# A hybrid decoder block on one core: head norms by transposes and row sums instead of a product with ones, and three sets of operands for the output's blocks

## The chip, the core and the metric

The kernel runs on one core of a Trainium2 chip. The metric is the device time of one execution in microseconds (us); the median of three runs is compared. TensorE is PE in the profile (PEld is its loading of stationary operands), VectorE DVE, ScalarE ACT, GpSimd POOL, and SyncE SP, which here only issues DMAs. Each engine takes its instructions in the order in which they stand in its queue.

## What is computed

One decoder block over 1024 tokens of 1024 channels, all in float32. After an RMSNorm, one input projection gives queries, keys, values and gates for two groups of heads. Eight heads of 64 channels do stick-breaking attention, four heads of 128 do a gated delta rule in chunks. Each head's output is normalised over its own channels, multiplied by a gate, and all of it goes through the output projection, a residual sum and a last RMSNorm. The change concerns the norm of the attention's heads and the output projection:

```python
o_sb = stick_breaking_attention(to_heads(sb_q, SB_HEADS, SB_HEAD_DIM), ...)
o_sb = rmsnorm(o_sb.transpose(0, 2, 1, 3), sb_norm_w[layer]).reshape(b, t_len, SB_WIDTH)
o_sb = o_sb * jax.nn.silu(sb_z)
...
mixed = jnp.concatenate([o_sb, o_gdn], axis=-1)
x = x + jnp.einsum('bte,ed->btd', mixed, w_out[layer])
return rmsnorm(x, final_norm_w)
```

Here rmsnorm(x, w) is x / sqrt(mean(x * x) + 1e-6) * w, the mean taken over the 64 channels of a head.

## The kernel before

**A planner sets the order.** The program is written as twelve generators (streams): projections, the four steps of the delta rule, attention, the output's weights, `factors`, `prepare`, `product` and others. `interleave` (L394) runs a model of the engines (class `Model`, L139) while the program is recorded: whenever TensorE's queue is empty in the model, it lets the ready stream of lowest priority number go on to its next `yield`. A stream yields either a condition (`lambda`) or an operation whose end it needs. So TensorE's queue is in the order of recording, and the queues of the other engines are in the order in which the model starts their instructions, by priority; both are fixed in the program (L1436 to L1439). Any change of an operation, a priority or a condition can move everything behind it. All operations pass through one recorder, so that the profile has the line L316 for nearly all of them and they are told apart by their tiles.

**Precision.** Large products are made of three passes (`mm3`, L517) over operands that are split in a high and a low part (xh and xl, weh and wel, woh and wol, mh and ml); their moving operand has up to 512 columns. The small products and the transposes take float32 operands as they are.

**Attention.** Heads are taken in pairs that share 128 partitions (64 rows of a tile each), and queries in pairs of blocks of 128 tokens. `pair(h, p)` (L1191) transposes the weights sg on TensorE with the identity (`ident`, a part of the tile step), multiplies them by the values into the bank po, and puts the output of head h for 256 tokens into half of the tile oe (128 rows of channels by 256 tokens) and into DRAM (o_s). After the second head of a pair (h odd) oe is squared on ScalarE, and a product with `sel` (128 x 128, two columns of ones over 64 rows each, the rest is not used for sums) gives the sums of squares over each head's 64 rows in two rows of a bank of the ring pz. VectorE turns them into mean plus epsilon in oe[0:2], and a DMA puts these two rows into DRAM (ss_s). That happens 16 times: four head pairs, four pairs of blocks.

**The factors.** `factors` (L1259) waits for a head pair's last sums (for the last head pair: for each pair of blocks), reads them from DRAM spread over 128 partitions (sst), takes the inverse square root by ten small steps on VectorE (`_rsqrt`, L45), and writes them back to DRAM (rs_s). That happens seven times: head pairs 0 to 2 once each with 16 columns, head pair 3 four times with 4 columns.

**The output stage.** It works on eight blocks of 128 tokens. `prepare` (L1336) makes a block's operands in two halves. The delta half (g = 1) transposes mx, the normed delta output that `mixed_delta` scaled on VectorE, and multiplies it by its gate. The attention half (g = 0) loads o_s (oa), the factors with a broadcast over 64 partitions (rb) and the gates (ga), multiplies rb by the gates on GpSimd (the fourth head pair's gate is still on chip as zt), and multiplies oa by that on VectorE (mf). Both halves end in mh (ScalarE) and ml (GpSimd). The operands of a block and its residual rows xr lie in one of two sets, in turn, so that block b waits for the end of block b - 2 (`f{b - 2}`, L1342). `product` (L1374) multiplies each block by the output weights in two parts of 512 columns (the last block in three) and eight slices of channels, adds the residual, and norms the result. The first two blocks' delta halves are multiplied before their attention halves. The output weights' rows 0 to 3 are split (woh, wol) once the last projection is done, since they lie where its operands were.

**Small things.** The constants conv, n1, mixw and others lie in the unused columns of sel. The delta group keeps its factors in rk, rq and rsg.

## Time and profile before

| | |
|---|---|
| median of three runs | 678.75 us (678.58 to 679.62) |
| the profiled execution's own time | 679.42 us |
| its span, first to last instruction | 677.6 us |
| TensorE busy | 655.8 us, 97% |
| VectorE busy | 480.1 us, 71% |
| ScalarE busy | 381.7 us, 56% |
| GpSimd busy | 327.0 us, 48% |
| DMA, mean share of the 16 engines | 47.1% |

A row of the profile that groups instructions has line, engine, operation, out<-in, shapes and count, then the time in which at least one of them ran, the mean duration in ns, and the idle time of the engine just ahead of them with what ended it. A row of a timeline has start and length in us, engine, line, operation, tiles, shape and count; a square bracket holds idle time ahead and its releaser. Matmuls are pipelined: one's duration overlaps the next, so what it costs the queue is the distance between starts.

### The profile page before, as it was taken

The page shows a single profiled execution, that of the slowest core. Times are in us where ns is not written, and L with a number is a line of the kernel's source. Part 1 is how long each engine was busy: PE and PEld are TensorE (multiplying, and loading weights), DVE is VectorE, ACT ScalarE, POOL GpSimd, SP SyncE. Part 2 cuts the span into 40 slices and gives each one's busy share as a digit, 9 for nine tenths or more (in the row PEclk, how much of TensorE's full clock was granted, in tenths as well). Part 3 has the DMA queues.
Part 4 walks back from the last instruction along what each step waited for, and adds up shares of the span by engine and source line. Part 5 has one row for each costly group of instructions (what it writes and reads, how often), then busy time and mean ns, then how long its engine had stood idle before and what let it go on. Part 6 is the DMA issues. An engine that isn't in the chain of part 4 may idle for free.

```text
span 677.6 us, 11750 instructions
## 1 busy us (share of the span) xinstructions
PE 655.8 (97%) x3998; PEld 557.8 (82%) x3998; DVE 480.1 (71%) x1007; ACT 381.7 (56%) x953; POOL 327.0 (48%) x301
## 2 busy tenths in 40 slices
PE   8999999999899989999999999999999999999995
PEld 6889987897788878788877888888888888877884
DVE  5354646425997866997598898997879964786643
ACT  5663138824797654966777684677858531322121
POOL 0002157527943677523797249863446444334331
PEclk9999999999899999999999999999999999999999
DMA  8928253546060555045433237253264755477431
GB/s 302 387 91 319 94 189 124 182 155 201 20 203 19 137 153 164 2 140 154 135 123 103 80 91 237 68 157 99 82 192 133 253 173 156 136 220 229 134 130 63
DMA packets 80972, 102.17 MB, mean 151 GB/s; under 512 B 17584, under 2 KB 49680, under 8 KB 80912
## 3 DMA queue, kind: packets, MB, share of 16 engines
q1 hardware_dynamic: 80912, 101.42, 47.1%
q8 instruction: 32, 0.52, 0.3%
q14 instruction: 28, 0.23, 0.1%
HBM read 73.50 MB, written 27.89 MB: 150 GB/s over the span
## 4 chain that ended last, share of the span: by engine, by line
PE 67%; POOL 12%; DVE 7%; ACT 5%; issue 5%; DMA 3%; SPq 1%; POOLq 0%; ACTq 0%; DVEq 0%
PE pp L316 39%; PE pz L316 19%; PE po L316 6%; POOL tm L316 6%; PE pc L316 3%; POOL wel L316 2%; POOL sg L316 2%; ACT pz L316 1%; DMA rb<-rs_s 1%; DVE cc L316 1%; DVE pp L316 1%; DVE pre L316 1%; ACT sg L316 1%; POOL kq L316 1%; SPq L316 1%
## 5 line engine op out<-in xcount | busy, mean ns | idle before, releaser
L316 PE MATMUL pp<-xh,weh 128*128 128x512 f32 x384 | 160.3, 417 | 3.8 <-DVE pre L316 3.8
L316 PE MATMUL pp<-xh,wel 128*128 128x512 f32 x384 | 151.0, 393 | 0.0
L316 PE MATMUL pp<-xl,weh 128*128 128x512 f32 x384 | 150.5, 392 | 0.0
L316 POOL TENSOR_TENSOR sg<-sg,cc 128x128 f32<-128x128 f32 (+3 forms) x64 | 77.1, 1209 | 63.6 <-DVE cc L316 37.2
L316 POOL TENSOR_TENSOR wel<-wer,weh 128x512 fp32r<-128x512 f32 x48 | 62.1, 1295 | 88.9 <-ACT weh L316 83.2
L316 PEld LDWEIGHTS pp<-xh,weh 128*128 128x128 f32 x384 | 72.4, 188 | 16.5 <-DVE pre L316 5.9
L316 PEld LDWEIGHTS pp<-xh,wel 128*128 128x128 f32 x384 | 72.2, 188 | 16.3
L316 PEld LDWEIGHTS pp<-xl,weh 128*128 128x128 f32 x384 | 72.6, 189 | 10.3
L316 POOL TENSOR_TENSOR tm<-xs,br 128x32 f32<-128x32 f32 (+7 forms) x64 | 59.2, 925 | 12.3 <-DVE xs L316 11.2
L316 ACT ACTIVATE ah<-pz 128x512 fp32r<-128x512 f32 (+1 forms) x80 | 43.5, 556 | 31.7 <-PE pz L316 30.8
L316 ACT ACTIVATE sg<-pz,sel 128x384 f32<-128x384 f32 (+3 forms) x96 | 53.8, 589 | 10.4 <-PE pz L316 9.3
L316 DVE TENSOR_TENSOR al<-pz,ah 128x512 fp32r<-128x512 f32 (+1 forms) x80 | 49.7, 630 | 10.3 <-ACT ah L316 9.9
L316 DVE TENSOR_TENSOR_SCAN cc<-pz,step 128x384 f32<-128x384 f32 (+2 forms) x64 | 53.1, 844 | 4.9 <-ACT pz L316 2.3
L316 ACT ACTIVATE pz<-pz,sel 128x384 f32<-128x384 f32 (+3 forms) x96 | 52.4, 565 | 0.1
L316 PE MATMUL pp<-chl,xh 128*128 128x264 f32 (+1 forms) x256 | 47.0, 285 | 0.8 <-DVE pre L316 0.8
L316 PE MATMUL pz<-step,sg 128*128 128x128 f32 x288 | 43.8, 275 | 2.4 <-DVE cc L316 1.7
L316 PE MATMUL po<-ah,v2a 128*128 128x256 f32 (+1 forms) x160 | 43.7, 297 | 0.0
L316 POOL TENSOR_TENSOR ml<-mf,mh 128x512 fp32r<-128x512 f32 x16 | 20.6, 1291 | 46.0 <-ACT mh L316 46.0
L316 DVE SCALAR_TENSOR_TENSOR pp<-pre,sel,pp 128x512 f32<-128x512 f32 x48 | 36.0, 749 | 9.6 <-ACT pp L316 8.9
L316 DVE TENSOR_REDUCE xs<-tm 128x16 f32<-128x32 f32 (+7 forms) x64 | 27.7, 432 | 18.5 <-POOL tm L316 18.0
L316 PEld LDWEIGHTS pp<-chl,xh 128*128 128x128 f32 x256 | 39.6, 188 | 1.2 <-DVE pre L316 1.0
L316 PE MATMUL pp<-woh,mh 128*128 128x512 f32 (+1 forms) x104 | 39.6, 381 | 0.6 <-ACT mh L316 0.6
(254 smaller groups left out, 1599.1 us busy)
## 6 DMA issues: line engine op xcount, KB each, us to landing
wer<-wE SPq DMA_DIRECT2D x48, 256.0 KB, 3.2
xr<-x SPq DMA_DIRECT2D x16, 512.0 KB, 8.6
qk_s<-xq SPq DMA_DIRECT2D x8, 512.0 KB, 4.8
v_s<-v2e SPq DMA_DIRECT2D x16, 256.0 KB, 2.0
q<-qk_s SPq DMA_DIRECT2D x8, 512.0 KB
kh<-qk_s SPq DMA_DIRECT2D x8, 512.0 KB
kl<-qk_s SPq DMA_DIRECT2D x8, 512.0 KB, 5.1
v2a<-v_s SPq DMA_DIRECT2D x8, 512.0 KB, 8.7
```

Of the source, the lines that this page charges most:

```text
L316: ins = f(*args, **kw).ins
```

## The change

The sums of squares: the product with sel, VectorE's evacuation of two rows and the DMA to ss_s go. In their place the squared oe is transposed in two pieces of 128 tokens, and one reduction on VectorE sums the 64 channels of each head and block into a tile that stays on chip, ssn (128 tokens by head pair, block and head). `factors` adds the mean and epsilon there, takes the inverse square root as before, transposes the result on TensorE (16 or 4 rows of 128 tokens), copies it out of the bank and writes it to rs_s. The load from ss_s goes.

```diff
                 sp = pz()[:, 0:256]
-                TE.matmul(sp, sel, oe, start=True, stop=True)
-                V.tensor_scalar(oe[0:2], sp[0:2], 1.0 / SBD, EPS, ALU.mult, ALU.add)
-                flags[f"t{h // 2}{p}"] = S.dma_start(ss_s[h // 2, p], oe[0:2])
+                for u in range(2):
+                    TE.transpose(sp[:, u * P:(u + 1) * P], oe[:, u * P:(u + 1) * P], ident)
+                flags[f"t{h // 2}{p}"] = V.tensor_reduce(ssn[:, h // 2, 2 * p:2 * p + 2, :].rearrange("p b u -> p (b u)"),
+                                                         sp.rearrange("p (n d) -> p n d", d=SBD), AX.X, ALU.add)
...
-                yield S.dma_start(ss, src)
-                _rsqrt(V, None, rs, ss, m, us)
-                r = S.dma_start(dst, rs)
+                ss = ssn[:, j, bl, :].rearrange("p b u -> p (b u)")
+                rs, us = rst[:, 0:m], ust[:, 0:m]
+                V.tensor_scalar(ss, ss, 1.0 / SBD, EPS, ALU.mult, ALU.add)
+                yield _rsqrt(V, None, rs, ss, m, us)
+                yield lambda: ps.room("pz", 4)
+                tp = pz()
+                TE.transpose(tp[0:m, 0:P], rs, ident)
+                V.tensor_copy(rsn[0:m], tp[0:m, 0:P])
+                r = S.dma_start(rs_s[j, bl].rearrange("b u t -> (b u) t"), rsn[0:m])
```

The output's blocks: a third set of operands lies in the tiles v2a and cc of attention. Block b waits for the end of block b - 3 instead of b - 2 (block 2 for the loaded last gain fnw instead of the end of block 0). A block's first product also waits, while the program is recorded, for attention's last output.

```diff
-                    yield lambda: b == 0 or "late" in flags and (b < 2 or f"f{b - 2}" in flags)
-                    pool = (pools[0], at_)[b % 2]
-                    xr = pool.tile([P, D], F32, **(dict(tag="cc", bufs=2) if b % 2 else dict(tag="xr")), name="xr")
+                    yield lambda: b == 0 or "late" in flags and (b < 2 or "fnw" in flags and (b < 3 or f"f{b - 3}" in flags))
+                    pool = at_ if b % 3 else pools[0]
+                    xr = pool.tile([P, D], F32, **(dict(tag="cc", bufs=2) if b % 3 else dict(tag="xr")), name="xr")
                     S.dma_start(xr, x_d[bs, :])
-                    mh = pool.tile([P, NK, P], F32R, tag=("mh", "kl")[b % 2], name="mh")
-                    ml = pool.tile([P, NK, P], F32R, tag=("ml", "q2")[b % 2], name="ml")
+                    mh, ml = [pool.tile([P, NK, P], F32R, tag=t, bufs=1 + (t == "v2a"), name="mh") for t in (("mh", "ml"), ("kl", "q2"), ("v2a", "v2a"))[b % 3]]
...
-                        yield lambda: ps.room(tag, bufs)
+                        yield lambda: f"e{SBH - 1}{NB // 2 - 1}" in flags and ps.room(tag, bufs)
```

The low part ml is now also named mh in the program's names. The rest makes room: sel becomes small (the constants alone, without memset and reduction), sst, ss_s, rsg and rk go; the delta group's last scaling is written into rq in place, and its key factor rr takes the place of mr2b, with nk computed ahead of mr2b.

How the queues move. TensorE, around the sums of the last head pair's last blocks (oe is the squared output, pp a projection's bank). Before:

```order
2519 L316 MATMUL pp_6731<-xl_109,weh_6561 128x512
2520 L316 MATMUL pp_6731<-xh_108,wel_6562 128x512
2521 L316 MATMUL pz_6761<-oe_6628,sel_66 128x256
2522 L316 MATMUL pp_6731<-xh_108,weh_6561 128x512
2523 L316 MATMUL pp_6731<-xl_109,weh_6561 128x512
2524 L316 MATMUL pp_6731<-xh_108,wel_6562 128x512
```

And now, where the transpose of the factors from these sums (rst) follows at row 2600:

```order
2573 L316 MATMUL pp_6846<-xl_105,weh_6716 128x512
2574 L316 MATMUL pp_6846<-xh_104,wel_6717 128x512
2575 L316 MATMUL pz_6876<-step_65,oe_6698 128x128 x2
2576 L316 MATMUL pp_6846<-xh_104,weh_6716 128x512
2577 L316 MATMUL pp_6846<-xl_105,weh_6716 128x512
2578 L316 MATMUL pp_6846<-xh_104,wel_6717 128x512
```

One product has become two transposes; between rows 2575 and 2600 stand 24 matmuls of projections.

TensorE in the output stage, at the transposes of block 2's delta half (mx; woh, wol with mh, ml are output products, po and pc the banks of block 0, pz that of block 1). Before:

```order
2689 L316 MATMUL pc_7028<-woh2_6981,ml_6658 128x512
2690 L316 MATMUL pc_7028<-woh3_6985,mh_6657 128x512
2691 L316 MATMUL pc_7028<-wol3_6986,mh_6657 128x512
2692 L316 MATMUL pc_7028<-woh3_6985,ml_6658 128x512
2693 L316 MATMUL pz_7112<-step_65,mx_6991 128x128 x4
2694 L316 MATMUL pz_7041<-woh0_6973,mh_6686 128x512
2695 L316 MATMUL pz_7041<-wol0_6974,mh_6686 128x512
2696 L316 MATMUL pz_7041<-woh0_6973,ml_6687 128x512
```

Now:

```order
2672 L316 MATMUL pz_7075<-woh6_6552,mh_6801 128x512
2673 L316 MATMUL pz_7075<-woh7_6577,mh_6800 128x512
2674 L316 MATMUL pz_7075<-wol7_6578,mh_6800 128x512
2675 L316 MATMUL pz_7075<-woh7_6577,mh_6801 128x512
2676 L316 MATMUL pz_7092<-step_65,mx_7012 128x128 x4
2677 L316 MATMUL po_7036<-woh0_6994,mh_6702 128x512
2678 L316 MATMUL po_7036<-wol0_6995,mh_6702 128x512
2679 L316 MATMUL po_7036<-woh0_6994,mh_6703 128x512
```

The four transposes stood behind the second half of block 0's products; they now stand ahead of it, 24 matmuls earlier.

SP's queue, at the last store of factors (rs_s) and the loads of block 2's attention half (the oa, rb and ga that follow the three pairs mx and gt). Before:

```order
377 L316 DMA gt_7008<-gate_s_91 128x4x128
378 L316 DMA rs_s_94<-rst_75 128x4
379 L316 DMA oa_7129<-o_s_92 128x4x128
380 L316 DMA rb_7130<-rs_s_94 64x4x128 x2
381 L316 DMA ga_7131<-gate_s_91 128x3x128
382 L316 DMA xr_7108<-x 128x1024
```

Now, with block 2's oa_7109, rb_7110 and ga_7111 next behind the last row:

```order
344 L316 DMA rs_s_90<-rsn_75 4x128
345 L316 DMA oa_6947<-o_s_89 128x4x128
346 L316 DMA rb_6948<-rs_s_90 64x4x128 x2
347 L316 DMA ga_6949<-gate_s_88 128x3x128
348 L316 DMA mx_7012<-og_s_91 128x512
349 L316 DMA fnw_7010<-fnw 128x1024
350 L316 DMA gt_7013<-gate_s_88 128x4x128
351 L316 DMA mx_7020<-og_s_91 128x512
352 L316 DMA gt_7021<-gate_s_88 128x4x128
353 L316 DMA mx_7028<-og_s_91 128x512
354 L316 DMA gt_7029<-gate_s_88 128x4x128
355 L316 DMA xr_7088<-x 128x1024
```

The store stood directly ahead of block 2's loads and now stands ahead of block 1's.

More of the change, by code (lines that the diff above doesn't have):

```diff
@@ L452, in block @@
         ident = step[:, 384:512]
-        sel = cst.tile([P, P], F32, name="sel")
-        conv = sel[:, 2:50].rearrange("p (a b) -> p a b", b=4)
-        n1, mixw, rstd, rs8, ns8, al2 = [sel[:, 50 + 8 * i:58 + 8 * i] for i in range(6)]
+        small = cst.tile([P, 96], F32, name="small")
+        conv = small[:, 0:48].rearrange("p (a b) -> p a b", b=4)
+        n1, mixw, rstd, rs8, ns8, al2 = [small[:, 48 + 8 * i:56 + 8 * i] for i in range(6)]
         alog, dtb = al2[:, 0:GH], al2[:, GH:]
@@ L458, in block @@
         make_identity(nc, ident)
-        V.memset(sel[:, 98:P], 0.0)
-        V.tensor_reduce(sel[:, 0:2], ident.rearrange("p (h d) -> p h d", h=2), AX.X, ALU.add)
-        sst, rst, ust = [cst.tile([P, 16], F32, name=n) for n in ("sst", "rst", "ust")]
+        rst, ust = [cst.tile([P, 16], F32, name=n) for n in ("rst", "ust")]
+        ssn = cst.tile([P, 4, NB, 2], F32, name="ssn")
+        rsn = cst.tile([16, P], F32, name="rsn")
         V.memset(step[:, 0:384], 0.0)
-        rsg = cst.tile([P, GH, NB], F32, name="rsg")
         ssg = cst.tile([P, GH, NB], F32, name="ssg")
-        rk = cst.tile([P, GH, NB], F32, name="rk")
         rq = cst.tile([P, GH, NB], F32, name="rq")
@@ L1261, in factors @@
                 yield from until(f"t{j}{p}")
+                bl = slice(0, NB) if j < 3 else slice(2 * p, 2 * p + 2)
                 m = 16 if j < 3 else 4
[L1263 to L1267 removed]
+                ss = ssn[:, j, bl, :].rearrange("p b u -> p (b u)")
[7 more added lines that the diff above has]
+                r = S.dma_start(rs_s[j, bl].rearrange("b u t -> (b u) t"), rsn[0:m])
                 for b in range(NB) if j < 3 else (2 * p, 2 * p + 1):
```

17 lines of the change are left out of this document (7 added, 10 removed).

## The prediction

> **What bounds the kernel now.** I read the page's first part, then the busy time by stretches, then the waits, and last the timeline of each engine around the two places that the change touches.
>
> ```profile
> PE 655.8 (97%) x3998; PEld 557.8 (82%) x3998; DVE 480.1 (71%) x1007; ACT 381.7 (56%) x953; POOL 327.0 (48%) x301
> ```
>
> ```profile
> 260.00:280.00 20.00, 19.79 (x146) 15.99 (x145) 16.62 (x29) 15.37 (x38) 12.32 (x11) 1.00 0.33 101
> 340.00:360.00 20.00, 19.18 (x106) 15.48 (x105) 19.22 (x32) 13.09 (x27) 19.31 (x16) 1.00 0.50 158
> ...
> 580.00:600.00 20.00, 20.00 (x92) 16.29 (x91) 16.60 (x40) 3.51 (x6) 5.40 (x5) 1.00 0.51 150
> 600.00:620.00 20.00, 18.63 (x81) 14.29 (x80) 14.16 (x35) 4.61 (x8) 7.93 (x8) 1.00 0.75 221
> 620.00:640.00 20.00, 20.00 (x93) 16.35 (x92) 13.31 (x30) 4.61 (x8) 7.18 (x8) 1.00 0.59 183
> ```
>
> The columns behind the stretch are the busy time of PE, PEld, DVE, ACT and POOL, then the granted clock. TensorE is busy for 655.8 of 677.6 us, and in nearly every stretch for over 19 of 20 us at full clock. There is no other bound to find: the span is TensorE's work plus the 21.8 us in which it has none. So there are two ways to make this kernel faster, and each part of the change is weighed by them: less work for TensorE counts in full wherever it lies, as the plan fills its queue with projections up to the output stage; and a wait of TensorE that goes counts in full. Work taken from VectorE, ScalarE or the DMA queue counts only where TensorE waits for it. The end, from TensorE's last matmul on, is untouched:
>
> ```profile
> 669.48 0.28 PE L316 MATMUL pp<-woh,ml 128*128 128x256 f32 x1
> ```
>
> That leaves 677.6 - 669.8 = 7.8 us of the 21.8 out of the change's reach, and some 14 us of idle time inside. VectorE comes close to TensorE in some stretches (19.22 of 20 at 340), which is where work moved to it could hurt.
>
> **The sums of squares, on TensorE.** Sixteen products with sel become 32 transposes. The product, and transposes of the same shape as the new ones, stand side by side in TensorE's timeline:
>
> ```profile
> 239.07 0.60 PE L316 MATMUL pz<-oe,sel 128*128 128x256 f32 x2
> 239.50 0.39 PE L316 MATMUL pc<-state,kq 128*128 128x128 f32 x2
> 239.72 0.49 PE L316 MATMUL pz<-step,sg 128*128 128x128 f32 x3
> ```
>
> ```profile
> L316 PE MATMUL pz<-step,sg 128*128 128x128 f32 x288 | 43.8, 275 | 2.4 <-DVE cc L316 1.7 <-ACT pz L316 0.4 <-POOL sg L316 0.3
> ...
> L316 PE MATMUL pz<-oe,sel 128*128 128x256 f32 x32 | 9.4, 387 | 1.9 <-ACT pz L316 1.8
> ...
> L316 DVE TENSOR_SCALAR oe<-pz 2x256 f32<-2x256 f32 x16 | 6.4, 405 | 2.7 <-PE pz L316 2.5
> ```
>
> One product is two records (x32 for 16) and holds the queue from 239.07 to 239.50: 0.43 us. Three transposes take 0.49 us, of which the last one's duration is 0.275; the two before it advanced the queue by 0.215, 0.11 us each. So 16 x 0.43 = 6.9 us go and 32 x 0.11 = 3.5 us come: 3.4 us saved. The seven new transposes of the factors are of the same kind (128 moving columns), 7 x 0.11 = 0.8 us. Net: **-2.6 us** of TensorE's work.
>
> The mean of the transposes' group, 275 ns, tempts to another price. In this trace it is a duration and not the distance to the next start, as the products' 387 ns is; the queue moves on after 0.11 us. The Trainium skill ("TensorE: Matmul & The Clock Gate", Part 4: PE-mode transpose) puts a 128x128 transpose in a kernel's context at about 275 ns; by it the change would cost TensorE 39 x 0.275 - 6.9 = 3.8 us where I count a gain of 2.6. The rows speak for the 0.11, and the duration as a price stays as a rival.
>
> **The sums, on VectorE.** The evacuation of 2x256 (0.405 us) becomes a reduction of 128x256 to 128x4. The nearest rows are a reduction of that size and a copy out of PSUM:
>
> ```profile
> 247.10 0.42 DVE L316 TENSOR_REDUCE xs<-tm 128x16 f32<-128x256 f32 x1 [0.97 <-POOL tm L316]
> ...
> 281.53 0.42 DVE L316 COPY w<-pz 32x256 f32<-32x256 f32 x1
> ```
>
> So 16 exchanges at about nothing. Each of the seven factor steps gets one small scalar operation more (0.15 to 0.17 us, like its neighbours in the chain below) and one copy from PSUM (0.42 at most): 7 x 0.6 = 4 us on an engine that is idle for 197 us. Cover: TensorE runs on matmuls that were issued before; if that cover is missing it is a wait of TensorE, counted next.
>
> **The new wait of TensorE.** A factor was computed from DRAM to DRAM beside TensorE. Now a transpose stands in TensorE's queue behind VectorE's steps, and everything after it (projections, the recurrence's small products, attention) waits if they are late. How long such steps take when VectorE is busy:
>
> ```profile
> 274.45 0.99 DVE L316 TENSOR_SCALAR rst<-sst 128x16 int32<-128x16 int32 x1
> ...
> 287.53 0.16 DVE L316 SCALAR_TENSOR_TENSOR rst<-ust,rst 128x16 f32<-128x16 f32 x1
> ```
>
> That is 13.2 us for ten small operations, since other work stands between them. In the new order the transpose for the first head pair stands 71 matmuls behind the last pair of oe transposes, 89 and 71 for the next two, and in the last head pair 83, 102, 105 and 26. At 146 records in the 20 us of the row 260:280, 71 are at least 9.7 us. The shortfall is between 0 and 13.2 - 9.7 = 3.5 us for each of the three chains inside attention. In the last pair little else stands between (the 26 are nearly all of 512 columns, 24 x 0.23 = 5.5 us, and the new VectorE order has one evacuation and then the chain without a break). The planner places the transpose where its own model has the steps done, so most should cost nothing; the nearest rows are TensorE's present waits for VectorE:
>
> ```profile
> PEld pz L316 <- DVE cc L316: 7.5, 15, 1.2
> ...
> PE pz L316 <- ACT pz L316: 2.2, 2, 1.8
> ```
>
> 0.5 us a time. I take one such, **+0.5 us**, between 0 and 10.5 (3 x 3.5).
>
> **The output stage.** Here TensorE waits visibly:
>
> ```profile
> 601.62 0.39 PE L316 MATMUL pp<-woh,ml 128*128 128x512 f32 x1
> 602.65 0.50 PE L316 MATMUL pp<-woh,mh 128*128 128x512 f32 x1 [0.64 <-ACT mh L316]
> 602.99 0.40 PE L316 MATMUL pp<-wol,mh 128*128 128x512 f32 x1
> 604.01 0.50 PE L316 MATMUL pp<-woh,ml 128*128 128x512 f32 x1 [0.63 <-POOL ml L316]
> 604.35 0.40 PE L316 MATMUL pp<-woh,mh 128*128 128x512 f32 x1
> 604.58 0.40 PE L316 MATMUL pp<-wol,mh 128*128 128x512 f32 x1
> ```
>
> Undisturbed, starts are 0.23 apart (604.35 to 604.58). From 601.62 to 604.35 there are four steps, 0.92 us, in 2.73: 1.8 us lost, on the operands of block 2. Followed back:
>
> ```profile
> 578.65 0.68 SPq L316 DMA_DIRECT2D gt<-gate_s  x1
> 588.89 0.32 SPq L316 DMA_DIRECT2D rs_s<-rst  x1
> 589.25 0.44 SPq L316 DMA_DIRECT2D oa<-o_s  x1
> 589.78 1.24 SPq L316 DMA_DIRECT2D rb<-rs_s  x2
> ```
>
> ```profile
> 578.80 6.19 DVE L316 SCALAR_TENSOR_TENSOR wol<-wor,sel,woh 128x1024 fp32r<-128x1024 f32 x4
> ...
> 588.71 0.15 DVE L316 SCALAR_TENSOR_TENSOR rst<-ust,rst 128x4 f32<-128x4 f32 x1
> ...
> 600.82 0.68 DVE L316 TENSOR_TENSOR mf<-oa,rb 128x512 f32<-128x512 f32 x1
> ```
>
> ```profile
> 596.60 0.46 POOL L316 TENSOR_TENSOR rb<-rb,zt 128x128 f32<-128x128 f32 x1
> 597.02 1.02 POOL L316 TENSOR_TENSOR rb<-rb,ga 128x384 f32<-128x384 f32 x1
> ```
>
> The store of the last factors waits on SP until 588.89, because its steps on VectorE stand behind the four splits of the output weights; block 2's loads stand behind that store, reach GpSimd at 596.60, and the product mf, whose inputs are there at 598.0, runs at 600.82, behind block 0's y. In the new order all of this moves ahead: the last factors are done before VectorE takes the first half of the last gate (z7), their store stands 11 issues ahead of block 2's loads instead of directly ahead of them, and block 2's transposes precede the second half of block 0's products, 24 matmuls or 5.5 us earlier. Since mf would then start over 5 us sooner and it was about 1.8 us late, that wait goes: -1.8 us. What is late next is block 2's transposes themselves. They need mx, scaled on VectorE right behind the splits:
>
> ```profile
> 576.02 0.39 PE L316 MATMUL po<-woh,mh 128*128 128x512 f32 x1
> ```
>
> ```profile
> L316 DVE TENSOR_SCALAR mx<-mx,rsg 128x128 f32<-128x128 f32 x32 | 13.1, 440 | 4.2 <-DMA mx<-og_s 4.2
> ```
>
> The splits end at 578.80 + 6.19 = 584.99; one mf product (0.68) and four scalings (13.1 / 32 = 0.41 each) follow, to 587.3. TensorE's output products begin at 576.02, and it comes to these transposes after 48 of them, 48 x 0.23 = 11.0 us, at 587.0. So some 0.3 us may be lost there, which the 0.5 us above, taken as one wait, is to hold as well. The third set matters for blocks 3 to 7, whose gate moves from the end of the block before last to the one before that; in the stretch 620:640 TensorE is busy for 20.00 of 20 us, so I count nothing.
>
> The rest is at nothing: the reused tiles (rr, rq), the swapped nk, and the missing setup of sel are VectorE's, before or beside TensorE's work; the 23 DMAs that go (16 stores, 7 loads) free SP. The gate on the last pair of attention would bind only if output products came before attention's end; the new order has them behind all projections, as before.
>
> **Sum**: -2.6 + 0.5 - 1.8 = **-3.9 us**. Against the profiled execution, 679.42 (span 677.6 and 1.8 around it), 675.5. The median of the three runs is 678.75, 0.67 lower: **674.9**. No change means within 0.2%, 1.4 us; the three runs lie 1.0 apart.
>
> **Rivals.**
> (a) *The plan falls better than counted.* Every row after some 260 us is dealt anew, and a wait like this one may go with it; it cost 1.84 us:
>
> ```profile
> 253.20 0.70 PE L316 MATMUL pz<-oe,sel 128*128 128x256 f32 x2 [1.84 <-ACT pz L316]
> ```
>
> About 2 us more: 672.8. For it: the product waits there only for a bank. Against: the transposes need that bank too. 0.10.
> (b) *The output stage keeps its wait*, in another place (mx behind the splits, or loads of three blocks at once, as the third set lets them crowd). Then -2.6 + 0.5: 676.7. 0.12.
> (c) *The new order gives it back.* Some 14 us of idle time lie inside the kernel, nearly all in attention and all set by small mistakes of the plan; a new plan has its own. A quarter more, 3.5 us: 678.4, no change. 0.14.
> (d) *TensorE waits for the factors*, slower. Place: the three transposes inside attention; price: up to 3.5 us each, 684.9 without my 0.5; it decides from (4.4 + 1.4)/3 = 1.9 us each. For it: 13.2 us before, VectorE at 19.22 of 20. Against: the chain starts without the trip through DRAM, and the planner puts the transpose behind it. 0.07.
> (e) *Transposes at their duration*: if each of the 39 holds the queue for the 0.275 us of its group's mean, TensorE's work grows by 10.7 - 6.9 = 3.8 us instead of shrinking by 2.6; with the other terms +2.5: 681.2. Against: 0.11 in the rows. 0.03.
>
> My forecast has 0.54. Faster: 0.54 + 0.10 + 0.12 = 0.76; same 0.14; slower 0.07 + 0.03 = 0.10. The range runs from a little under (a) to a little over (c): 671.5 to 678.9.
>
> **What would show it.** Right: some 653 us busy on PE; oe's transposes advancing by 0.11; no wait over 0.3 us on mh between the first output product and the last; the tail still 7.8 us. Wrong: gaps of PE ahead of transposes of rst, or a sum of idle time inside that is over 14 us though both places look as forecast.

## The result and the profile after

The changed kernel takes **690.8 us** (median of 6 runs, 688.33 to 692.51) beside 678.66 us for the kernel before (6 runs on the same chip, 678.12 to 679.88): ratio 1.0173, 95% interval 1.0148 to 1.0198. It is slower by 12 us, where 674.9 was forecast. The profiled execution of the changed kernel is the quickest of its six: 688.33 us, span 686.4, against 677.6 before.

The first part of its page:

```profile
PE 656.3 (96%) x4005; PEld 555.4 (81%) x4005; DVE 471.3 (69%) x1019; ACT 381.1 (56%) x953; POOL 330.0 (48%) x301
```

TensorE is as busy as before (655.8) in a span that is 8.8 us longer. To see where, the program is cut into four stretches: the part ahead of the largest effects, the part in which attention and the delta recurrence run together, the rest of attention, and the output's blocks. Busy time by stretches, the changed kernel (columns: PE, PEld, DVE, ACT, POOL, granted clock, DMA share, GB/s):

```profile
0.00:320.00 320.00, 309.87 (x1961) 266.32 (x1962) 205.66 (x454) 189.23 (x484) 140.91 (x136) 1.00 0.48 159
320.00:440.00 120.00, 113.54 (x753) 95.41 (x752) 93.94 (x208) 84.30 (x241) 84.50 (x80) 1.00 0.39 119
440.00:580.00 140.00, 139.03 (x863) 116.76 (x862) 111.00 (x219) 84.33 (x190) 69.31 (x56) 1.00 0.47 153
580.00:660.00 80.00, 74.54 (x328) 60.41 (x327) 50.16 (x105) 19.59 (x30) 32.50 (x29) 0.96 0.56 174
```

The same stretches of the kernel before:

```profile
0.00:320.00 320.00, 309.72 (x1953) 266.86 (x1954) 207.93 (x453) 189.47 (x486) 141.72 (x136) 0.99 0.49 160
320.00:440.00 120.00, 118.01 (x774) 99.21 (x773) 100.28 (x202) 84.05 (x234) 84.72 (x80) 1.00 0.41 121
440.00:580.00 140.00, 139.72 (x861) 119.62 (x860) 109.40 (x206) 88.90 (x199) 71.14 (x57) 1.00 0.51 157
580.00:660.00 80.00, 78.63 (x351) 63.28 (x350) 55.89 (x124) 16.28 (x28) 26.70 (x26) 1.00 0.55 168
```

Two stretches lose: 4.5 us of TensorE's time between 320 and 440 us (113.54 for 118.01), and 4.1 us at the output's blocks (74.54 for 78.63), where the clock is lower as well. The other two are level within 0.7 us.

**The output's blocks.** The timeline around 610 to 621 us of the changed kernel:

```profile
609.27 1.25 SPq L316 DMA_DIRECT2D rb<-rs_s  x2
...
614.52 0.39 PE L316 MATMUL pp<-woh,mh 128*128 128x512 f32 x1
...
617.71 0.45 POOL L316 TENSOR_TENSOR rb<-rb,zt 128x128 f32<-128x128 f32 x1 [6.23 <-DMA rb<-rs_s]
618.12 0.99 POOL L316 TENSOR_TENSOR rb<-rb,ga 128x384 f32<-128x384 f32 x1
619.14 0.69 DVE L316 TENSOR_TENSOR mf<-oa,rb 128x512 f32<-128x512 f32 x1 [6.79 <-POOL rb L316]
619.98 0.69 DVE L316 TENSOR_TENSOR y<-pp,xr 128x512 f32<-128x512 f32 x1
620.65 0.68 DVE L316 TENSOR_TENSOR y<-pp,xr 128x512 f32<-128x512 f32 x1
...
620.82 0.76 PE L316 MATMUL pp<-woh,mh 128*128 128x512 f32 x1 [5.46 <-DVE ry L316]
```

Read it from the last row back. TensorE stands for 5.46 us, since both pp banks hold block 2's product. The view puts this wait down to ry, a small step of VectorE right behind the first addition (620.59), and the wait of the weight load there to mh on ScalarE (620.78, 5.67 us); that it is the bank was a reading at this point, and the run e3 below bears it out. VectorE frees the banks with the two additions y<-pp, whose sums were complete when the product's last matmul ended at 614.9. But ahead of them in VectorE's queue stands mf<-oa,rb, and it is block 4's: with three sets the preparation of block 4 may be ordered before block 2 has left PSUM. That mf waits for GpSimd, which waits for the load of the factors, issued at 609.27 and in use at 617.71. The kernel before has a similar pattern one block milder, in VectorE's timeline:

```profile
607.76 0.68 DVE L316 TENSOR_TENSOR y<-pp,xr 128x512 f32<-128x512 f32 x1
612.65 0.54 DVE L316 TENSOR_SCALAR mx<-mx,rsg 128x128 f32<-128x128 f32 x1 [4.20 <-DMA mx<-og_s]
613.14 0.69 DVE L316 TENSOR_TENSOR mf<-oa,rb 128x512 f32<-128x512 f32 x1
...
614.33 0.69 DVE L316 TENSOR_TENSOR y<-pp,xr 128x512 f32<-128x512 f32 x1
```

There VectorE stands 4.20 us for a late load of mx, and behind it comes block 3's mf, whose factors GpSimd had ready only at 613.1. Both stand behind the first of block 2's additions: one bank was free from 608.4 on, and TensorE had work for it. The third set moves an mf of one block later in ahead of both additions.

The gap costs more than its length. The granted clock around the gap and behind it:

```profile
614.00:620.50 6.50, 1.35 (x8) 0.90 (x7) 1.34 (x3) 0.63 (x1) 1.40 (x2) 0.77 0.61 202
620.50:624.50 4.00, 3.68 (x9) 2.94 (x10) 4.00 (x14) 1.78 (x3) 1.38 (x2) 0.51 0.25 58
```

The nine records from 620.82 on take 3.68 us at 0.51; undisturbed starts are 0.23 us apart, which would make 2.07 us. Some 1.6 us more are lost.

**The attention.** The largest new wait is at 359.80:

```profile
357.83 0.69 DVE L316 TENSOR_TENSOR pre<-pp,rbc 128x512 f32<-128x512 f32 x1
...
359.00 0.74 DVE L316 SCALAR_TENSOR_TENSOR pre<-pre,small,pp 128x512 f32<-128x512 f32 x1
...
359.80 0.50 PE L316 MATMUL pp<-xh,weh 128*128 128x512 f32 x1 [3.33 <-DVE pre L316]
```

A projection waits for a bank that VectorE's convolution steps (pre, pp) hold. No transpose of the factors is near: their first chain (the small steps of one inverse square root on VectorE) begins at 266.28 and its result is copied at 278.08, the second begins at 384.11.

```profile
266.28 0.65 DVE L316 TENSOR_SCALAR ssn<-ssn 128x16 f32<-128x16 f32 x1
...
278.08 0.28 DVE L316 COPY rsn<-pz 16x128 f32<-16x128 f32 x1
...
384.11 0.15 DVE L316 TENSOR_SCALAR ssn<-ssn 128x16 f32<-128x16 f32 x1
```

### The profile page after: what moved, and what is told of

Read it like the earlier page. It is cut to its first block, busy times and chain, and to the rows that moved or that the text cites. A ratio compares the mean times of both kernels' runs of the same rounds, so it can differ in the third digit from the quotient of the medians.

```text
span 686.4 us, 11700 instructions
## 1 busy us (share of the span) xinstructions
PE 656.3 (96%) x4005; PEld 555.4 (81%) x4005; DVE 471.3 (69%) x1019; ACT 381.1 (56%) x953; POOL 330.0 (48%) x301
## 4 chain that ended last, share of the span: by engine, by line
PE 65%; DVE 10%; POOL 9%; ACT 8%; issue 4%; DMA 3%; SPq 0%; POOLq 0%; DVEq 0%; ACTq 0%
PE pp L316 38%; PE pz L316 18%; PE po L316 5%; POOL tm L316 5%; PE pc L316 3%; ACT pz L316 2%; DVE cc L316 2%; DVE pp L316 1%; POOL wel L316 1%; POOL sg L316 1%; DMA rb<-rs_s 1%; DVE pre L316 1%; DVE xs L316 1%; ACT pp L316 1%; DVE al L316 1%
## 5 line engine op out<-in xcount | busy, mean ns | idle before, releaser
L316 PE MATMUL pp<-woh,mh 128*128 128x512 f32 (+1 forms) x208 | 62.9, 384 | 5.5 <-DVE ry L316 5.5
L316 ACT ACTIVATE sg<-pz,small 128x384 f32<-128x384 f32 (+3 forms) x96 | 53.4, 585 | 11.4 <-PE pz L316 10.4
L316 ACT ACTIVATE pz<-pz,small 128x384 f32<-128x384 f32 (+3 forms) x96 | 52.1, 561 | 0.0
L316 PEld LDWEIGHTS pp<-woh,mh 128*128 128x128 f32 x208 | 38.9, 192 | 13.7 <-ACT mh L316 5.7
L316 DVE SCALAR_TENSOR_TENSOR pp<-pre,small,pp 128x512 f32<-128x512 f32 x48 | 36.0, 750 | 7.3 <-ACT pp L316 6.9
L316 DVE TENSOR_TENSOR_SCAN cc<-pz,cc,step 128x512 f32<-128x512 f32 (+1 forms) x32 | 38.6, 1207 | 3.0 <-ACT pz L316 2.8
```

Source lines behind the costliest of these rows:

```text
L316: ins = f(*args, **kw).ins
```

## The experiments

**Theory A**, formed on these rows: two separate losses, one of the third set at the output's blocks (VectorE's order), one of the plan in the attention, dealt anew. Against it stood: the whole loss is the norms' (B), or the third set's (C); that three blocks' loads crowd the queues whatever the order (D); and that the new operations themselves cost the attention (E).

### One half at a time, and the order of one multiply

e1: the changed kernel with the sets and gates of before.

```diff
-                    yield lambda: b == 0 or "late" in flags and (b < 2 or "fnw" in flags and (b < 3 or f"f{b - 3}" in flags))
...
+                    yield lambda: b == 0 or "late" in flags and (b < 2 or f"f{b - 2}" in flags)
...
+                    mh = pool.tile([P, NK, P], F32R, tag=("mh", "kl")[b % 2], name="mh")
+                    ml = pool.tile([P, NK, P], F32R, tag=("ml", "q2")[b % 2], name="ml")
...
-                        yield lambda: f"e{SBH - 1}{NB // 2 - 1}" in flags and ps.room(tag, bufs)
+                        yield lambda: ps.room(tag, bufs)
```

> Norms by transposes with the two sets of operands of before: TensorE's order is that of the changed kernel word for word up to the output's blocks, and the stage of the blocks is built as in the kernel before. Theory A (two losses add: about 4 us net in the attention, where the order is dealt anew, and about 5 us at the output's blocks, where the third set lets a later block's multiply stand ahead of the copy out of PSUM): the 5.5 us gap of TensorE near 620 is gone, the 3.3 us gap near 360 stays; 682 to 685 us, 3.5 to 6 us over the kernel before and 5 to 8 under the changed one. Rival B (the third set is innocent, the whole loss lies in the norms): as the changed kernel, 688 to 691. Rival C (the whole loss is the third set's): 675 to 677, below the kernel before.

e2: the kernel before with the same lines changed the other way round.

> Three sets of operands with the product with sel as before: TensorE's order is that of the kernel before word for word up to the output's blocks. Theory A: the attention as before (stalls of TensorE before 560 us 23 us in all), at the output's blocks a gap of TensorE of 3 to 6 us behind the multiply of block 4 on VectorE, which stands between the two copies out of PSUM of block 2 here; 681 to 686 us. Rival B (third set innocent): 677 to 679. Rival C: 684 to 690.

e3: the changed kernel, in which the multiply mf of blocks 3 to 7 is held back until the second addition y<-pp of the block two ahead (the flag y) is done:

```diff
                 else:
+                    if b > 2:
+                        yield from until(f"y{b - 2}")
                     V.tensor_tensor(fv, oa.rearrange("p j t -> p (j t)"), rb.rearrange("p j t -> p (j t)"), ALU.mult)
...
+                        if n == 1:
+                            flags[f"y{b}"] = r
```

> The changed kernel, with the multiply of the attention's half (mf from oa and rb) of blocks 3 to 7 issued only once the block two ahead has been copied out of PSUM; the three sets and the early loads stay. Theory A (it is the place in VectorE's queue): the gap of 5.5 us near 620 and the slow clock behind it go, 681 to 684 us, 6 to 9 under the changed kernel. Rival D (three blocks' loads at once crowd the DMA queues, whatever the order): TensorE then waits for block 4's operands some 10 us later, 687 to 691 us.

Measured, beside 677.88 for the kernel before: e1 683.68 (ratio 1.0082, 1.0062 to 1.0102), e2 681.30 (1.0052, 1.0033 to 1.0072), e3 683.15 (1.0081, 1.0058 to 1.0105). Neither half bears all: B and C fall. The stretches 320:440 and 580:660 of e1:

```profile
320.00:440.00 120.00, 115.03 (x747) 97.04 (x747) 92.32 (x204) 82.77 (x236) 83.42 (x78) 0.97 0.37 114
...
580.00:660.00 80.00, 78.74 (x352) 63.49 (x351) 57.04 (x115) 18.98 (x31) 30.98 (x28) 1.00 0.59 179
```

and of e3:

```profile
320.00:440.00 120.00, 114.49 (x738) 97.19 (x739) 90.54 (x202) 81.44 (x232) 81.46 (x77) 0.96 0.36 112
...
580.00:660.00 80.00, 80.00 (x360) 65.11 (x359) 57.91 (x116) 20.13 (x31) 33.58 (x31) 1.00 0.58 183
```

In e1 the output's blocks are as before (78.74) and the attention loses as in the changed kernel: TensorE's queue is the changed kernel's up to the output's blocks, and the wait of 3.3 us is there (3.36, at 357.86). At a clock of 0.97, part of e1's busy time is at half rate, so the loss is more than the 3 us of idle time. In e3 TensorE is busy for 80.00 of 80 us at the output's blocks, with three sets and the loads as early as in the changed kernel: D falls, it is the place of mf in VectorE's queue. In e2 the loss is at the output's blocks alone (76.02 of 80, and 117.96 of 120 between 320 and 440), but its longest wait comes by one step more:

```profile
617.51 0.59 SPq L316 DMA_DIRECT2D out<-y  x1
...
624.38 0.69 DVE L316 TENSOR_TENSOR y<-pp,xr 128x512 f32<-128x512 f32 x1 [3.86 <-DMA ga<-gate_s]
...
625.22 0.47 PE L316 MATMUL pp<-woh,mh 128*128 128x512 f32 x1 [3.98 <-DVE y L316]
```

There mf (613.45) had delayed block 2's second addition to 614.06. SP's queue has a load of xr, which waits for that addition, ahead of block 1's output (617.51), and block 3's addition at 624.38 seems to wait for block 1's y to be stored; the view names another DMA, so this last link is argued.

### The old order played back

e4: norms as in e1; the planner's choices of the kernel before are recorded and played back, stream by stream.

```diff
 def interleave(ck, room, streams):
...
-    while streams:
...
+    every = list(streams)
+    for i in DEAL:
+        s = every[i]
+        while ck.pe or not ((room() or s.prio >= 100 or s.prio < 0) and s.ready(ck)):
...
             ck.advance()
```

DEAL holds the 2135 choices of the kernel before. The wait for a free bank of pz ahead of the factors' transpose goes as well.

> Norms by transposes, two sets, and the planner's choices of the kernel before played back, so that TensorE's order is that of before but for the 39 transposes in the place of the 16 products. Theory A (the attention's loss comes of the new deal, not of the new operations): the terms of the forecast hold, TensorE 2.6 us less, waits within 1 us of before: 675 to 677.5 us. Rival E (the new operations cost it: VectorE's reductions, the waits of TensorE for the factors): 680 to 684 us, with gaps of TensorE at the transposes of oe and rst of over 3 us in all.

711.07 us (ratio 1.0475, 1.0451 to 1.0500), far outside both. The playback put the transposes of the factors where their loads had been, ahead of their chain on VectorE. Its waits and the longest one in the timeline:

```profile
PE pz L316 <- DVE rst L316: 19.6, 3, 8.8
```

```profile
411.15 1.54 POOL L316 TENSOR_TENSOR sg<-sg,cc 128x768 f32<-128x768 f32 x1 [2.35 <-DVE cc L316]
411.23 1.50 DVE L316 TENSOR_TENSOR ust<-ust,ssn 128x16 f32<-128x16 f32 x1
...
420.64 0.38 PE L316 MATMUL pz<-step,rst 128*16 128x128 f32 x1 [8.80 <-DVE rst L316]
```

So this run doesn't tell A from E; it prices the wait that rival (d) of the prediction spoke of, where the order leaves no room for the chain: up to 8.8 us each.

e5: the same with the factors' stream left out of the list and served when it is ready.

> As the run that played the choices of before back, but the stream of the factors (the reciprocal roots and their seven transposes) is left free: it is served whenever its operands are there and TensorE's plan is empty, so that no transpose of rst is put ahead of its VectorE chain. Theory A (the loss there was the played-back place of the factors, 19.6 us of waits for rst, and the attention's loss in the changed kernel is the deal's): no wait of TensorE over 1 us at rst; 675 to 679 us. Rival E (head norms on VectorE cost the attention by their own operations): 681 to 688 us.

690.76 (1.0177, 1.0147 to 1.0206): A's 675 to 679 is missed, and E's 688 is exceeded. TensorE is busy for 111.26 of 120 us in 320:440. The queues of VectorE and ScalarE were still dealt anew here, which leaves the run open to either reading.

### Other deals of the order

e6, e11: the kernel before; e7, e8: the norms of e1. One constant of the planner is nudged (PORT 60 to 65 in e6 and e7, TO_PE 70 to 65 in e8 and e11), no instruction changes. PORT is the planner's extra price in ns when VectorE and GpSimd meet at their shared port, TO_PE what it adds to an operation's end before TensorE may use the result. e10: the norms of e1 with `return 215 if args[1].tensor.name.startswith("oe") else 108` as the price of a transpose.

> The kernel before with one constant of the planner nudged (the price of a shared port 65 ns in place of 60): no instruction changes, only the order from the attention on. Theory A (each deal of the order is a draw with a spread of some us): within 4 us of the kernel before, and not within 0.5; rival E (deals are alike, so 4 us more must come from the operations): 677 to 679.

> Norms by transposes with two sets, dealt anew by the same nudge (65 for 60). Theory A: another draw, the gap of 3.3 us near 360 is gone or elsewhere; 676 to 684 us. Rival E: 682 to 685 again.

> Norms by transposes with two sets, dealt anew by another nudge (the planner's hop to TensorE 65 ns in place of 70). Theory A: another draw, 676 to 684 us, over 1 us from at least one of the other two deals with these norms. Rival E: 682 to 685 again.

> Norms by transposes, two sets, with the planner told that a transpose of oe takes 215 ns in place of 108, so that two cost what the product cost (430): no instruction changes, only the plan. Theory A (a deal like any other): 676 to 685. If the loss comes because the planner sees 0.2 us less of TensorE's work at each norm and so pulls the next products forward: within 1 us of 676. Rival E: 682 to 686.

> The kernel before, dealt anew by the nudge that e8 had (the hop to TensorE 65 ns in place of 70). If the deals of before spread as those of the norms might: 680 to 685, 2 us or more above the kernel before. If the product with sel leaves a plan that holds under nudges, as with the other nudge (e6: 679.0 beside 678.0): 677 to 680.

| kernel | us | ratio to before, 95% | PE busy in 320:440 |
|---|---|---|---|
| before | 677.9 to 679.5 | 1 | 118.01 |
| before, e6 | 678.97 | 1.0005 (0.9990 to 1.0019) | 117.86 |
| before, e11 | 676.80 | 0.9982 (0.9970 to 0.9994) | 119.42 |
| norms, e1 | 683.68 | 1.0082 (1.0062 to 1.0102) | 115.03 |
| norms, e7 | 683.83 | 1.0084 (1.0053 to 1.0115) | 115.53 |
| norms, e8 | 684.79 | 1.0097 (1.0070 to 1.0124) | 114.24 |
| norms, e10 | 681.39 | 1.0046 (1.0030 to 1.0063) | 117.82 |

Theory A's second half loses most of its ground: the three runs of the kernel before lie within 2.2 us of each other (e11 a little below both of its ranges), and the four runs of the norms all lie 3 to 7 us above it. How much of this is a new deal is read by comparing the queues in the traces. TensorE's order in e6 is that of the kernel before up to 426 us, and in e7 that of e1 up to 382 us; e11 leaves the kernel before at 339 us, and e8 and e10 leave e1 at 331 and 240 us. So in the main there are, between 320 and 440 us, two orders of the kernel before (118.01, 119.42) and three of the norms (115.03, 114.24, 117.82). A spread of deals exists: e10 is 2.3 us under e1 and loses nothing in that stretch, but 1.97 us between 440 and 580 (137.75 for 139.72). None of the norms' orders comes down to the kernel before; something in the norms costs time in each of them.

### The cause in the attention: the factors

e9: as e5, with the queues of VectorE, ScalarE, GpSimd and SP played back too, instruction by instruction. (The recorder's line is L454 in e9, e12 and e16.)

```diff
     def start(self, eng):
...
+        heads, script = self.heads[eng], self.script[eng]
+        first = next((h for h in heads if script and h[2].key == script[0]), None)
+        first = first or min((h for h in heads if h[2].key not in self.told), default=None)
...
-        op = heapq.heappop(self.heads[eng])[2]
+        heads.remove(first)
+        op = first[2]
```

> Norms by transposes, two sets, with the order of the kernel before played back on every engine: TensorE's by the planner's choices, and the queues of VectorE, ScalarE, POOL and the DMA issues instruction by instruction; only the factors' chain and its seven transposes are put in freely. In e5 the order of VectorE and ScalarE was still dealt anew (ScalarE had 258 instructions in other places). Theory A (the loss of the attention is the order, the operations do what the forecast said): stalls of TensorE between 320 and 440 us back to 5 to 6 us from 10; 674.5 to 677.5 us, below the kernel before. Rival E (the operations cost it in any order): 680 to 686.

680.99 (1.0048, 1.0032 to 1.0065): within E's range, 3.5 us above A's. With the old order on every engine what is left must come of what was exchanged. Its timeline shows where:

```profile
411.87 0.27 PE L454 MATMUL pz<-step,rst 128*16 128x128 f32 x1
411.92 0.68 DVE L454 TENSOR_TENSOR kt<-pp,rbc 128x512 f32<-128x512 f32 x1
412.51 1.27 DVE L454 TENSOR_TENSOR_SCAN cc<-pz,cc,step 128x512 f32<-128x512 f32 x1
...
413.84 0.49 PE L454 MATMUL pz<-state,kq 128*128 128x128 f32 x2 [1.71 <-DVE cc L454]
413.88 1.21 DVE L454 TENSOR_TENSOR_SCAN cc<-pz,step 128x512 f32<-128x512 f32 x1
415.01 0.25 DVE L454 COPY rsn<-pz 16x128 f32<-16x128 f32 x1
```

The transpose takes one of the four pz banks at 411.87. The copy that frees it comes at 415.01, behind three large operations of VectorE: one bank less for 3.4 us, and meanwhile the next product into pz waits 1.71 us for a bank. During a second one, 489.05 to 491.76, there is a wait of 1.02 us (until 491.65).

Theory F: the factors inside the attention cost it. Rival G: the transposes of oe and the reductions do. e12: e9 with the factors put off; e13: e1 with that; e14: e13 with TO_PE 65; e15: e3 with that. In place of seven chains, three of them inside the attention, there are four, each of 16 columns (two blocks of all four head pairs), and they begin behind 515 us.

```diff
-            for j, p in [(0, 3), (1, 3), (2, 3)] + [(3, p) for p in range(4)]:
-                yield from until(f"t{j}{p}")
...
+            for p in range(4):
+                for j in range(4):
+                    yield from until(f"t{j}{p}")
+                bl = slice(2 * p, 2 * p + 2)
+                ss = ssn[:, bl, :, :].rearrange("p b j u -> p (b j u)")
...
+                yield _rsqrt(V, None, rst, ss, 16, ust)
```

> The run with the old order on every engine (e9), with the factors put off: in place of seven chains, three of them in the attention, four chains of 16 columns at the end, each once a pair of blocks has all its sums. Theory F (the factors cost the attention: their small operations on VectorE's queue and the PSUM bank that their transpose holds until the copy, 1.7 us at 414 and 1.0 at 492): the stalls of TensorE between 400 and 520 us go back from 6.5 to some 3 us; 674.5 to 678 us. Rival G (the transposes of oe and the reduction cost it): 679.5 to 682, as e9.

> Norms by transposes, two sets, factors put off to the end in four chains, order dealt by the planner. Theory F: 674 to 680 us, 3 us or more under the norms as changed (683.7). Rival G: 681 to 686.

> The same, dealt anew by the nudge that e8 and e11 had (hop 65 for 70). Theory F: 674 to 680 us. Rival G: 681 to 686.

> Norms by transposes, factors put off, and three sets of operands with the late multiply of e3. Theory F: within 2 us of e13, and below the kernel before by up to 3 us if TensorE waits nowhere at the output's blocks; 674 to 679. Rival G: 681 to 686.

| kernel | us (before: 679.48) | ratio, 95% | PE busy in 320:440 |
|---|---|---|---|
| e12 | 676.09 | 0.9959 (0.9940 to 0.9977) | 117.66 |
| e13 | 678.14 | 0.9974 (0.9959 to 0.9989) | 118.04 |
| e14 | 677.73 | 0.9986 (0.9971 to 1.0001) | 118.07 |
| e15 | **674.59** | 0.9937 (0.9914 to 0.9959) | 118.05 |

Theory F holds in the old order: apart from the factors' own operations e9 and e12 have the same queues on every engine, and the ratios lie 0.9% apart, 6 us. The two waits are 2.7 us of these 6; where the rest lies is not shown. Theory F fits the planner's own order too, but there it is tried in one order and not in three. The nudge of e14 moved nothing: its queues are those of e13 on every engine, so it repeats e13 (its interval reaches 1), and e15 has e13's order up to the output's blocks. That this one order is a lucky deal is not excluded; beside it stand the three orders with early factors. With the factors put off the attention is as before, and the transposes of oe and the reductions (G) cost it nothing.

The kernel before also has three chains inside its attention, and e12 has none, so e12 could gain by their absence. e16 asks this: e9 with the three early chains left on VectorE, and only the transposes, copies and stores put off. Theory F1 is that the bank counts which the transpose holds, F2 that the small operations on VectorE do.

> The old order on every engine as in e9 and e12. The three VectorE chains of the factors stand in the attention as in e9, their results are kept (a copy of 16 columns more each), and only the transposes, the copies out of PSUM and the stores are put off to the end. Theory F1 (the bank of PSUM that the transpose holds behind VectorE's queue): 675.5 to 678 us, as e12. Theory F2 (the small operations on VectorE's queue): 679.5 to 682, as e9.

Its time, 682.60 (1.0072, 1.0047 to 1.0097), lies above both ranges, nearer to F2's; the places of the waits speak for the bank (F1). The stretch 400:520 of e9:

```profile
400.00:520.00 120.00, 116.35 (x794) 100.12 (x794) 98.34 (x200) 85.01 (x220) 70.03 (x63) 1.00 0.42 130
```

of e12:

```profile
400.00:520.00 120.00, 119.07 (x809) 103.15 (x808) 96.66 (x182) 87.08 (x224) 74.76 (x65) 1.00 0.45 139
```

and of e16, with the wait in which its time went instead:

```profile
400.00:520.00 120.00, 119.14 (x793) 103.29 (x793) 98.86 (x199) 85.82 (x221) 70.92 (x62) 0.97 0.42 130
```

```profile
606.23 0.45 POOL L454 TENSOR_TENSOR rb<-rb,zt 128x128 f32<-128x128 f32 x1 [6.71 <-DMA rb<-rs_s]
...
609.23 0.79 PE L454 MATMUL pp<-woh,mh 128*128 128x512 f32 x1 [4.34 <-ACT mh L454]
```

The busy time of 119.14 us is not the proof that it looks like: e16 ran at half clock from 461 to 468 us (granted clock 0.51), so that its 793 records are no more than e9's 794. What counts is the time between the same two places of the queue, here from four transposes of sg to four later ones, across e9's first wait. It is 84.6 us in the kernel before (341.21 to 425.83), 86.4 in e9 (341.66 to 428.04), 84.1 in e12 (339.28 to 423.38) and 84.5 in e16 (341.30 to 425.81). With the chains there and the transposes gone, e16 has neither of e9's two waits, and over this stretch it takes as long as the kernel before. So in these places it is the transposes with their copies and not the chains; that they act by the bank is read from e9's timeline. The half clock and the 4.34 us at 609, a late load of the factors at the output's blocks, make up the run's total, so that the total decides nothing.

e17: the changed kernel with the factors put off and nothing else; e18: e15 with TO_PE 65.

> The changed kernel with its three sets and its order of the output's blocks, the factors put off as in e13, without the late multiply of e15; block 4's multiply of oa and rb stands right ahead of block 2's two copies out of PSUM on VectorE again. If the output stage's loss stands by itself: a gap of TensorE of 3 to 6 us at about 610, 678 to 683 us, 4 to 8 over e15. If it needs the attention's late end: no gap, 674 to 676.

> As e15 (norms by transposes, factors put off, three sets, late multiply), dealt anew by hop 65 for 70. 673 to 677 us if e15 is no lucky deal; 678 or more if it is.

e17 takes 678.38 us (1.0014, 0.9988 to 1.0041) beside 678.05, e18 675.77 (0.9960, 0.9935 to 0.9985). In e17 the attention is as before:

```profile
320.00:440.00 120.00, 118.09 (x782) 100.30 (x781) 97.95 (x202) 85.27 (x240) 86.27 (x81) 1.00 0.38 117
```

The output's loss stands by itself, with a gap of 2.58 us (3 to 6 were expected); its timeline:

```profile
608.48 0.69 DVE L316 TENSOR_TENSOR mf<-oa,rb 128x512 f32<-128x512 f32 x1 [3.65 <-POOL rb L316]
...
609.57 0.69 DVE L316 TENSOR_TENSOR y<-pp,xr 128x512 f32<-128x512 f32 x1 [0.27 <-DMA out<-y]
...
610.41 0.47 PE L316 MATMUL pp<-woh,mh 128*128 128x512 f32 x1 [2.58 <-DVE y L316]
```

The ratios of e15 and e17 lie 0.8% apart, 5 us, for the place of one multiply of a block in VectorE's queue. e18 was to show whether e15 is a lucky deal and doesn't: its queues are those of e15 on every engine, so it is a repetition. Both runs lie below the kernel before (0.9937 and 0.9960) and below the norms alone (e13 and e14, 0.9974 and 0.9986): with the factors put off and the multiply held back, both parts of the change gain in this order.

## Why the prediction was wrong

- **TensorE's work, -2.6 us: right.** Two transposes of oe advance the queue by 0.10 us each (252.42 to 252.61 in the changed kernel). In e12, the nearest to "the norms alone", TensorE is busy for 652.7 us (655.8 before; some 653 was forecast), and the time is 0.41% (2.8 us) lower. The changed kernel's own 656.3 holds the half rate behind its gap, 1.6 us. Rival (e) is refuted.
- **The sums on VectorE, and the reused tiles, at nothing: right.** A reduction takes 0.412 us in the mean, where the evacuation took 0.405; e12 has all of these edits and is below the kernel before.
- **The new wait of TensorE, +0.5 us: the step that failed first.** I priced the transposes of the factors only by how long TensorE would wait *at* them, and found the planner would leave room. It does: no wait stands at rst in the changed kernel. What I left out is everything that they do elsewhere. In the old order (e9) it is the bank of pz that they hold until VectorE gets to the copy. In the changed kernel's own order the three early ones hold theirs for 0.6, 0.7 and 1.2 us only, and the loss stands in other places. The norms as changed cost +5.8 us (e1) where -2.6 + 0.5 was summed: with TensorE's work as forecast, the term is 5.8 + 2.6 = 8.4 us, not 0.5. That it lies inside my outer bound of 10.5 is luck, as the mechanism is another one; rival (d) had the right operations and the wrong place.
- **The output stage, -1.8 us: right in its place.** The wait on block 2's operands is gone in e3, e15 and e18 (80.00 of 80 us busy). With two sets it stays (78.74 in e1, as before 78.63), so it is the third set that takes it away and not the earlier factors; in busy time it is 1.4 us.
- **"The third set matters for blocks 3 to 7 ... so I count nothing": the step that failed second.** I asked whether TensorE waited for operands there, and not what earlier operands would be put ahead of in VectorE's queue. The rows at 612.65 and 613.14 of the kernel before, late loads ahead of an addition, could have told me. Taking the changed kernel and e1 each against its own runs of before (12.1 and 5.8 us), the set cost 6.3 us; by e3 (5.3 us over before) the place of mf is worth 6.9. Rival (b) named a wait at this stage, for other reasons, and at 1.8 us.
- **The tail, 7.8 us:** 7.1 in the changed kernel (span 686.4, last matmul at 679.04 + 0.28); nothing hung on it.
- **The signs I gave for "wrong":** gaps at rst did not appear in the changed kernel. Idle time inside was 23 us instead of 14 (686.4 - 656.3 - 7.1), and one of the two places, the output's blocks, did not look as forecast. Of the signs for "right", "no wait over 0.3 us on mh" failed by the view's name for the weight load's wait (5.67 us), behind which stands the bank.

Open is how the factors bring about the stalls near 322 and 360 us in the changed kernel's own order, where none is under way. The stall near 360 is there in e1 and e7 too (3.36 and 3.32 us), whose order is the same in that place, and not in e13, e14, e15, e17 and e18, which share one order in the attention; in e8 and e10 the loss lies elsewhere or is smaller. The step from early factors to these stalls is not shown, nor is it excluded that the planner's one order without them is a good draw. What is shown in a fixed order is e9 against e12 and e16.

## What to carry to other kernels

When a transpose or a product replaces a trip through DRAM, price the PSUM bank from the moment TensorE writes it until the busy engine copies it out (3.4 us in e9), and do such steps where that engine has time. When a further buffer lets work start earlier, look in the order at what that work now stands ahead of on each in-order queue: an instruction that waits for a slow load, ahead of one that frees PSUM, hands the load's delay on to TensorE (5.46 us here). If a plan's luck is suspected, deal it again with a nudge, before and after, and compare the queues to see that the nudge moved something: of six nudges here two changed nothing (e14, e18), and two only what lies behind 426 and 382 us (e6, e7).

## What the runs showed of the hardware

**The clock after a gap.** The same wait, 3.3 us at 359.80, in two kernels with the same order there. The changed kernel:

```profile
359.80:361.00 1.20, 1.20 (x7) 1.02 (x8) 1.17 (x2) 0.61 (x1) 1.20 (x2) 1.00 0.00 0
361.00:365.00 4.00, 4.00 (x27) 3.30 (x26) 3.78 (x8) 3.15 (x8) 2.27 (x4) 1.00 0.41 134
```

and e3:

```profile
359.80:361.00 1.20, 1.20 (x3) 1.01 (x4) 1.16 (x2) 0.61 (x1) 1.20 (x2) 0.50 0.00 0
361.00:365.00 4.00, 4.00 (x17) 3.60 (x16) 3.14 (x6) 2.66 (x7) 1.60 (x2) 0.50 0.42 133
```

One keeps its clock, the other runs at half for over 5 us (17 records in 4 us for 27). So a gap of this size has two prices some 2.5 us apart. The changed kernel, which has two gaps of over 3 us, spreads over 4.2 us in its six runs where the kernel before spreads over 1.8; the quickest has a mean granted clock of 0.992, the slowest 0.985. That the spread comes of this is likely, but not shown gap by gap. The Trainium skill ("TensorE: Matmul & The Clock Gate", Part 1) has the array go to half rate after about 3.4 us without work, counted in a window that runs free; the halved clock and its chance nature agree, but in e17 a gap of 2.58 us was enough (clock 0.58 in 611.9 to 615.9). In e16 the clock was at half from 461 to 468 us (0.51) though the timeline ahead of it, from 452 us on, lists no wait of TensorE.

**Small operations beside GpSimd.** In e4 a VectorE multiply of 128x16, whose median is 0.17 us in the changed kernel (nine of them), took 1.50 us while GpSimd's multiply of 128x768 ran (411.15 to 412.69), and ended 0.04 us after it. The Trainium skill ("SBUF — State Buffer", Terms: shared port pair) has one of the two engines wait for the whole instruction of the other; the row agrees.

**The load of the factors** at the output's blocks, 64 partitions reading the same rows, was in use 8.4 us after its issue in the changed kernel (609.27 to 617.71), 5.4 in e15 (604.04 to 609.46) and 10.2 in e16 (596.06 to 606.23). The planner counts 1.1 us to its begin and 1.5 us behind its end, so an operation that waits for such a load can stand in VectorE's queue for much longer than the plan has it.
